# A decoder layer on one core: late operand loads on ScalarE's DMA queue, and plain output copies in ScalarE's fixed order

## The chip, the cores and the metric

The kernel runs on one core of a Trainium2 chip: TensorE (PE), VectorE (DVE), ScalarE (ACT), GpSimd (POOL) and SyncE (SP), which here only issues DMAs. The metric is the device time of one execution in microseconds (us), the median of several runs. Engine names in the profile have a q behind them (SPq, ACTq) where the row is of the engine's instruction queue, such as the issue of a DMA.

## The reference

One decoder layer on 512 tokens, model width 2048, hidden width 5632, all in float32:

```
h = rmsnorm(x);  u, v, q, k, v_att, g_a, g_b = split(h @ W_in)
y_a = u * (tril(W_s) rmsnorm(v) + b)          # in chunks of 128 tokens
y_b = stick_breaking_attention(q, k, v_att)
x  += (sigmoid(g_a) * (y_a @ W_up_a) + sigmoid(g_b) * (y_b @ W_up_b)) @ W_o
x  += (silu(h2 @ W_gate_in) * (h2 @ W_up_in)) @ W_out      # h2 = rmsnorm(x)
x  += sigmoid(rmsnorm(x) @ W_pg) * (p @ W_ple)
```

## The kernel before

**Products.** Everything is kept transposed: a block is 128 partitions (features) by 1024, two tiles of 128 features by 512 tokens side by side. A float32 operand is split into a high and a low part in fp32r, and a product takes three matmuls, high x high, high x low, low x high (`mm3`, L296 to L298). Most products are Strassen products of 2 x 2 blocks with seven multiplications (L701); others are "plain", with eight (L296 to L298). One output block is a *pair* (`Pair`): its products run in PSUM over all operands of the stage and are then combined.

**Operands.** Each stage reads operands that are made once: a float32 block is loaded, ScalarE copies it to the high part (L286; with the norm's gain L548 or L529), VectorE subtracts to get the low part (L287, L549), and for a Strassen operand VectorE also forms sums of its quarters (L534), which are split in the same way. A `plain_form` makes its four plain parts first, so that the first pairs can run as plain products, and loads the block a second time for the sums; a `late_form` makes what its first pair needs. Operands of the later stages come from spilled blocks in HBM: `y_spill` (attention's output, for W_up), `mix` (for W_o), `x1` (for the FFN's input), `hid` (for the FFN's output, in three passes of 8, 8 and 6 blocks) and `x2` (for the last gate). They are fetched by `load` (L523 to L526), whose DMA is L525, on SP's queue. So are the blocks that are read as they are: xT, the spilled gates (gsp), ple, and x1 and x2 for the residual sums.

**Stages** by time: W_in up to about 800 us, W_up to 1025, W_o to 1160, the FFN's input to 2020, its output in three passes to 2180, 2345 and 2465, the last gate to 2645. While the last pair of a stage is computed, the operands of the next one are built.

**Weights.** SP loads each weight block (L339 plain; L341 and L349 for Strassen) into one of a few landings, GpSimd adds two blocks by an accumulating DMA (L370), ScalarE copies the high part (L366), VectorE subtracts the low part (L363) and forms sums (L382). Three slots of high and low parts (whi0 to whi2, wlo0 to wlo2) go round. A landing is free when L363 has read it.

**What sets the order.** A scheduler places the instructions of each engine, with two bounds. `in_turn` chains the instructions given to it in a fixed order on their engine: the weights' L366, L363 and L382, and most of what combines an output. `tick` keeps the instructions of a step behind the newest chained instruction of ScalarE, VectorE and TensorE. SP has no such chain but for its weight loads among themselves (`asked`), so that a load of L525 on SP may stand far ahead of the step that asked for it. `Pair.out` (L793 to L800) copies a plain pair's two PSUM banks to SBUF on ScalarE (L799), outside the chain; a Strassen pair's copies (L724, L757) are in it.

**The start** (L873 to L936): `ple_raw` loads p in two halves on ScalarE's queue (L876), then ScalarE loads its function table (L922), TensorE warms up (L927), SP loads three w_ple blocks (L339), the first block of x (L919) and the gains.

Of the kernel before, what the change touches and what calls it, by code (L numbers as in the profile page):

```python
# [14 lines left out]
AF = mybir.ActivationFunctionType  # L15
# [5 lines left out]
T = 512  # L21
# [49 lines left out]
def hybrid_layer(  # L71
# [18 lines left out]
    nc = tc.nc  # L90
# [358 lines left out]
    def plain_weights(src):  # L449
        return Weights(src.rearrange("p (b c) -> p b c", b=4), 1, "P")  # L450
# [69 lines left out]
    def cut(x):  # L520
        return x.rearrange("p (b c) -> p b c", c=256)

    def load(src, n=1024, how="old"):  # L523
        b = take(n, how)
        nc.sync.dma_start(out=b.f(0, 1024), in_=src)  # L525
        return b  # L526

    def gained(dst, src, gi, k):
# [91 lines left out]
    def plain_form(src, ready=always, gain=None, raw=1024, how="low", far=False):  # L620
        def steps(form):
            hi, lo = form.blocks = parts.take(1024, how), parts.take(1024, how)
            w = form.raw()
            if gain:
                gained(hi.own(), w.f(), *gain)
                gi, k = gain
                for i in range(2):
                    a, b = i * T, (i + 1) * T
                    nc.vector.scalar_tensor_tensor(
                        out=lo.own(a, b), in0=w.f(a, b),  # L630
                        scalar=gcol[:, gi + 2 * k + i : gi + 2 * k + i + 1], in1=hi.f(a, b),
                        op0=ALU.mult, op1=ALU.subtract)
            else:
                split_into(hi.own(), lo.own(), w.f())
            give(w)
            return tuple([x.own(0, T), x.own(T)] for x in form.blocks)
            yield

        return Form("P", steps, [(parts, 1024, how)] * 2 + [(wholes, raw, "low")] * bool(raw),
                    ready, src, far)  # L640

    class Pair:
# [150 lines left out]
        def out(self, o=None):  # L793
            if self.n["S"]:
                assert o is None
                return self.rest(self.o)
            o = wide() if o is None else o
            for i, ps in enumerate(self.ends()):
                nc.scalar.activation(o[:, i * T : (i + 1) * T], ps, AF.Copy)  # L799
            return o  # L800

        def rest(self, o):
# [67 lines left out]
    ple_spill = {}  # L870
    ps_p = []

    def ple_raw(queue):  # L873
        raw = take(1024, "old")
        for k in (0, T):
            queue.dma_start(out=raw.f(k, k + T), in_=pT[:, k : k + T])  # L876
        return raw

    def ple_operands(raw=None):
        first = raw is not None  # L880
        raw = raw or ple_raw(nc.sync)
        ps_p.extend(parts.take(1024, "high") for _ in range(2))
        for k in (0, T):
            ops = split_into(*(x.own(k, k + T) for x in ps_p), raw.f(k, k + T))
            if first:
                in_turn(*ops)
        give(raw)
# [30 lines left out]
        x_raw.append(take(1024, "old"))  # L918
        nc.sync.dma_start(out=x_raw[-1].f(), in_=xT[len(x_raw) - 1])  # L919

    p_raw = ple_raw(nc.scalar)
    nc.scalar.preload_act_table_set("natural_log_exp_and_others")  # L922
    ones = consts.tile([P, P], F32, name="ones")
    nc.vector.memset(ones, 1.0)
    warm = small_bank()
    for _ in range(7):
        nc.tensor.matmul(warm[:, :P], ones, ones, start=True, stop=True)  # L927
    w_early = [plain_weights(w_ple[i]) for i in range(3)]
    load_x()
    gcol = consts.tile([P, ng], F32, name="gcol")  # L930
    nc.sync.dma_start(out=gcol, in_=gains)
# [384 lines left out]
            plan(w_gate[j], now(GATE, GATE_UNTIL, j))  # L1316

    def y_form(c, i):
        return plain_form((lambda: y_a[i]) if c == "a" else lambda: load(y_spill[i]),
                          lambda: len(y_done) == 8, raw=0 if c == "a" else 1024,  # L1320
                          far=c == "b")

# [40 lines left out]

    def spilled_form(kind, n, j, gain=None, **how):
        return (late_form if kind == "S" else plain_form)(
            lambda size=1024: load(spill[n, j], size), lambda: (n, j) in there, gain, far=True,
            **how)

    def store(n, j, block):
# [235 lines left out]
```

## Time and profile before

| | |
|---|---|
| median of 3 runs | 2656.03 us (2655.14 to 2657.5) |
| the profiled execution | 2652.22 us |
| its span in the trace | 2650.5 us, granted clock 0.999 |
| ScalarE busy | 1409.0 us |
| GpSimd busy | 451.5 us |
| DMA queue of SP | 440.77 MB, 50.6% of 16 engines' span |
| DMA queue of GpSimd | 117.47 MB, 27.8% |
| DMA queue of ScalarE | 0.52 MB, 0.1% |

A row of the waits names who waited, at which line, for what, then the total, the number of times and the longest. A row of a timeline has the start in us, the length (of all of them where xN follows), the engine, the line, the operation, out<-in, the form, and in brackets the idle time before it and what ended it. Line numbers are those of the kernel before.

### The profile page before, as it was taken

How to read it: one execution, taken by the hardware profiler on the slowest of the kernel's cores; microseconds unless marked ns; L12 is line 12 of the kernel's file. 1: busy time of each engine (PE TensorE's matmuls, PEld its weight loads, DVE VectorE, ACT ScalarE, POOL GpSimd, SP SyncE). 2: the span in 40 equal slices, each digit the busy share in tenths (PEclk: the TensorE clock that was granted, in tenths of full speed). 3: DMA queues.
4: the chain of work that ended last, by engine and by line, in shares of the span. 5: the costliest groups of instructions: out<-in, count | busy, mean ns of one | idle time of the engine just before them, and what ended most of it. 6: DMA issues, size and time to landing. Idle time of an engine off the chain costs nothing.

```text
span 2650.5 us, 42355 instructions
## 1 busy us (share of the span) xinstructions
PE 2635.0 (99%) x15202; PEld 2301.7 (87%) x15202; DVE 2255.1 (85%) x3856; ACT 1409.0 (53%) x2245; POOL 451.5 (17%) x559
## 2 busy tenths in 40 slices
PE   9999999999999999999999999999999999999999
PEld 7888888889998888888888888888888888889888
DVE  8687878787887558999888888888889989989898
ACT  7756565655554335466444444444445445455543
POOL 0222223232220001101111111111110211211010
PEclk9999999999999999999999999999999999999999
DMA  6777777677775669988888788888887989988794
GB/s 209 183 195 171 194 172 192 171 192 191 175 195 186 223 224 271 254 246 212 223 213 217 197 203 203 195 212 201 202 203 225 255 227 275 225 242 254 239 269 137
DMA packets 288130, 561.46 MB, mean 212 GB/s; under 512 B 26288, under 2 KB 133552, under 8 KB 287920
## 3 DMA queue, kind: packets, MB, share of 16 engines
q1 hardware_dynamic: 225856, 440.77, 50.6%
q0 software_dynamic: 61776, 117.47, 27.8%
q8 instruction: 119, 1.95, 0.3%
q14 instruction: 91, 0.75, 0.1%
q10 hardware_dynamic: 288, 0.52, 0.1%
HBM read 507.28 MB, written 51.38 MB: 211 GB/s over the span
## 4 chain that ended last, share of the span: by engine, by line
PE 94%; DVE 3%; ACT 1%; DMA 1%; issue 1%; SPq 0%; DVEq 0%; ACTq 0%
PE ps L701 56%; PE ps L298 9%; PE ps L297 9%; PE ps L296 9%; PE small L701 6%; DVE wlo L363 1%; PE small L1181 1%; PE small L1129 1%; PE small L1055 1%; DVE parts L287 1%; DVE wholes L534 0%; DVE wholes L382 0%; PE small L1240 0%; DMA wholes<-x 0%; DMA wholes<-w_ffn_out 0%
## 5 line engine op out<-in xcount | busy, mean ns | idle before, releaser
L701 PE MATMUL ps<-parts,whi 128*128 128x512 f32 x4390 | 1470.6, 398 | 1.9 <-DVE out L806 0.8
L366 ACT ACTIVATE whi<-wholes 128x512 fp32r<-128x512 f32 (+2 forms) x934 | 873.1, 948 | 759.4 <-DVE wholes L382 308.6
L363 DVE TENSOR_TENSOR wlo<-wholes,whi 128x512 fp32r<-128x512 f32 (+2 forms) x934 | 980.8, 1086 | 78.5 <-ACT whi L366 77.6
L701 PEld LDWEIGHTS ps<-parts,wlo 128*128 128x128 f32 x4390 | 823.9, 188 | 188.0 <-DVE wlo L363 2.5
L701 PE MATMUL ps<-parts,wlo 128*128 128x256 f32 x4390 | 868.4, 279 | 1.1 <-DVE wlo L363 1.1
L701 PEld LDWEIGHTS ps<-parts,whi 128*128 128x128 f32 x4390 | 707.2, 189 | 11.3 <-issue 3.1
L297 PE MATMUL ps<-parts,whi 128*128 128x256 f32 (+1 forms) x1622 | 538.4, 332 | 1.0 <-DVE parts L287 0.9
L298 PE MATMUL ps<-parts,wlo 128*128 128x256 f32 (+1 forms) x1622 | 538.3, 333 | 1.1 <-DVE wlo L363 1.1
L296 PE MATMUL ps<-parts,whi 128*128 128x256 f32 (+1 forms) x1612 | 532.5, 332 | 1.8 <-ACT parts L286 1.4
L382 DVE TENSOR_TENSOR wholes<-wholes 128x256 f32<-128x256 f32 x820 | 346.3, 422 | 15.8 <-DVE wlo L363 0.4
L760 DVE TENSOR_TENSOR out<-out,ps 128x256 f32<-128x256 f32 x525 | 216.8, 416 | 152.2 <-ACT out L757 152.0
L297 PEld LDWEIGHTS ps<-parts,whi 128*128 128x128 f32 x1622 | 305.9, 189 | 37.9 <-DVE parts L287 2.9
L298 PEld LDWEIGHTS ps<-parts,wlo 128*128 128x128 f32 x1622 | 306.2, 189 | 30.6 <-DVE wlo L363 1.5
L296 PEld LDWEIGHTS ps<-parts,whi 128*128 128x128 f32 x1612 | 303.5, 189 | 32.2 <-ACT parts L286 2.2
L370 POOL DMA_DIRECT2D wholes<-w_ffn_in x169 | 147.6, 873 | 704.2 <-DVE wholes L382 209.7
L370 POOL DMA_DIRECT2D wholes<-w_in x132 | 117.0, 888 | 543.1 <-DMA wholes<-w_in 112.3
L701 PE MATMUL small<-parts,whi 128*128 128x512 f32 x480 | 190.2, 397 | 0.0
L757 ACT ACTIVATE out<-ps 128x256 f32<-128x256 f32 x279 | 104.7, 385 | 57.0 <-PE ps L701 52.9
L287 DVE TENSOR_TENSOR parts<-wholes,parts 128x1024 fp32r<-128x1024 f32 (+3 forms) x139 | 124.0, 904 | 12.6 <-ACT parts L286 12.5
L286 ACT ACTIVATE parts<-wholes 128x1024 fp32r<-128x1024 f32 (+3 forms) x139 | 107.8, 797 | 46.5 <-DVE wholes L534 32.4
L370 POOL DMA_DIRECT2D wholes<-w_ffn_out x64 | 55.9, 873 | 356.0 <-DMA wholes<-w_ffn_out 84.7
L1428 ACT ACTIVATE out<-out 128x512 f32<-128x512 f32 x44 | 27.9, 633 | 156.2 <-DVE out L1427 156.2
(135 smaller groups left out, 1833.6 us busy)
## 6 DMA issues: line engine op xcount, KB each, us to landing
wholes<-w_ffn_in SPq DMA_DIRECT2D x169, 384.0 KB, 5.6
wholes<-w_in SPq DMA_DIRECT2D x132, 384.0 KB, 5.0
wholes<-w_ffn_in SPq DMA_DIRECT2D x169, 256.0 KB, 4.8
wholes<-w_ffn_in POOLq DMA_DIRECT2D x169, 256.0 KB, 5.4
wholes<-w_in SPq DMA_DIRECT2D x132, 256.0 KB, 4.1
wholes<-w_in POOLq DMA_DIRECT2D x132, 256.0 KB, 5.0
wholes<-w_ffn_out SPq DMA_DIRECT2D x64, 384.0 KB, 6.0
wholes<-x SPq DMA_DIRECT2D x46, 512.0 KB, 6.1
```

What stands on the lines that cost most here:

```text
L286: return (nc.scalar.activation(hi, src, AF.Copy), nc.vector.tensor_tensor(out=lo, in0=src, in1=hi.bitcast(F32), op=ALU.subtract))
L287: nc.vector.tensor_tensor(out=lo, in0=src, in1=hi.bitcast(F32), op=ALU.subtract))
L296: nc.tensor.matmul(ps, sh, mh, start=start, stop=False)
L297: nc.tensor.matmul(ps, sh, ml, start=False, stop=False)
L298: return nc.tensor.matmul(ps, sl, mh, start=False, stop=stop)
L363: in_turn(nc.vector.tensor_tensor(out=self.lo[:, blocks], in0=r, in1=h.bitcast(F32), op=ALU.subtract))
L366: in_turn(nc.scalar.activation(h, r, AF.Copy))
L370: nc.gpsimd.dma_start(out=raw[:, 3:5], in_=self.src[:, 1:3], accum_op=ALU.add)
L382: in_turn(nc.vector.tensor_tensor(out=o, in0=x, in1=y, op=ALU.add))
L701: m = nc.tensor.matmul(out, l, r, start=first and k == 0, stop=last and k == 1)
L757: in_turn(nc.scalar.activation(out, x, AF.Copy, scale=scale))
L760: in_turn(nc.vector.tensor_tensor(out=out, in0=x, in1=y, op=op))
```

## The change

Three edits:

```
-    def load(src, n=1024, how="old"):
+    def load(src, n=1024, how="old", queue=nc.sync):
         b = take(n, how)
-        nc.sync.dma_start(out=b.f(0, 1024), in_=src)
+        queue.dma_start(out=b.f(0, 1024), in_=src)
...
-        return plain_form((lambda: y_a[i]) if c == "a" else lambda: load(y_spill[i]),
+        return plain_form((lambda: y_a[i]) if c == "a" else lambda: load(y_spill[i], queue=nc.scalar),
...
-            lambda size=1024: load(spill[n, j], size), lambda: (n, j) in there, gain, far=True,
+            lambda size=1024: load(spill[n, j], size, queue=nc.scalar), lambda: (n, j) in there, gain, far=True,
```

The 92 loads of y_spill, mix, x1, hid and x2 that make operands go to ScalarE's queue; the other loads of L525 stay on SP.

```
             for i, ps in enumerate(self.ends()):
-                nc.scalar.activation(o[:, i * T : (i + 1) * T], ps, AF.Copy)
+                in_turn(nc.scalar.activation(o[:, i * T : (i + 1) * T], ps, AF.Copy))
```

The 16 copies of L799 that go through ScalarE for eight plain pairs join ScalarE's chain.

```
-    def ple_raw(queue):
+    def ple_raw(*queues):
         raw = take(1024, "old")
-        for k in (0, T):
-            queue.dma_start(out=raw.f(k, k + T), in_=pT[:, k : k + T])
+        for k, q in zip((0, T), queues):
+            q.dma_start(out=raw.f(k, k + T), in_=pT[:, k : k + T])
...
-    p_raw = ple_raw(nc.scalar)
+    w_early = [plain_weights(w_ple[0])]
+    p_raw = ple_raw(nc.scalar, nc.sync)
...
-    w_early = [plain_weights(w_ple[i]) for i in range(3)]
+    w_early.extend(plain_weights(w_ple[i]) for i in range(1, 3))
```

At the start the second half of p is loaded by SP, behind the first w_ple block; the second use of `ple_raw`, in the middle of the kernel, keeps both halves on SP.

What the scheduler makes of it. First ScalarE where the operands of the first hid pass are made (2011 to 2024 us), before; whi are weights' high parts, parts are operands, out and p5 are PSUM copies of an output.

```order
L366 ACTIVATE whi0_75<-wholes_74 128x512
L366 ACTIVATE whi2_79<-wholes_74 128x1280
L366 ACTIVATE whi2_79<-wholes_74 128x512
L366 ACTIVATE whi1_77<-wholes_74 128x1024
L286 ACTIVATE parts_73<-wholes_74 128x4x256 x3
L366 ACTIVATE whi0_75<-wholes_74 128x1024
L757 ACTIVATE out_1727_18757<-ps_1711_18637 128x256
```

And changed:

```order
L366 ACTIVATE whi2_79<-wholes_74 128x1280
L525 DMA wholes_74<-hid_1164_10912 128x1024
L366 ACTIVATE whi2_79<-wholes_74 128x512
L525 DMA wholes_74<-hid_1165_10913 128x1024
L366 ACTIVATE whi1_77<-wholes_74 128x1024
L525 DMA wholes_74<-hid_1166_10914 128x1024
L286 ACTIVATE parts_73<-wholes_74 128x4x256
L366 ACTIVATE whi0_75<-wholes_74 128x1024
L525 DMA wholes_74<-hid_1167_10915 128x1024
L286 ACTIVATE parts_73<-wholes_74 128x4x256
L525 DMA wholes_74<-hid_1168_10916 128x1024
L286 ACTIVATE parts_73<-wholes_74 128x4x256
```

The loads of the first five blocks now stand among ScalarE's weight copies of that stretch, each behind the copy before it, and the second and third operand's L286 stand behind the copy to whi0 that they preceded.

SP, before, in the FFN's input stage, where the load of the first hid block is issued at 1221.9 us (hid_10912 on the left is a store of it, on the right the load):

```order
L349 DMA wholes_74<-w_ffn_in 128x768
L1431 DMA hid_1164_10912<-out_1257_11121 128x512
L341 DMA wholes_74<-w_ffn_in 128x2x256
L349 DMA wholes_74<-w_ffn_in 128x768
L525 DMA wholes_74<-hid_1164_10912 128x1024
L341 DMA wholes_74<-w_ffn_in 128x2x256
L349 DMA wholes_74<-w_ffn_in 128x768
```

and in the changed kernel the same stretch of weight loads:

```order
L341 DMA wholes_74<-w_ffn_in 128x2x256
L1432 DMA hid_1164_10912<-out_1257_11121 128x512
L349 DMA wholes_74<-w_ffn_in 128x768
L341 DMA wholes_74<-w_ffn_in 128x2x256
L349 DMA wholes_74<-w_ffn_in 128x768
L341 DMA wholes_74<-w_ffn_in 128x2x256
L349 DMA wholes_74<-w_ffn_in 128x768
```

The load of hid has left it; what remains are weights and the stores of L1431 (L1432).

TensorE, in the first pair of the first hid pass (ps_1739 and ps_1740 are the two banks of its output, whi0 and wlo0 the parts of its weight), before:

```order
L296 MATMUL ps_1739_18816<-parts_73,whi0_75 128x512
L297 MATMUL ps_1739_18816<-parts_73,whi0_75 128x512
L298 MATMUL ps_1739_18816<-parts_73,wlo0_76 128x512
L296 MATMUL ps_1739_18816<-parts_73,whi0_75 128x512
L297 MATMUL ps_1739_18816<-parts_73,whi0_75 128x512
L298 MATMUL ps_1739_18816<-parts_73,wlo0_76 128x512
L296 MATMUL ps_1740_18817<-parts_73,whi0_75 128x512
L297 MATMUL ps_1740_18817<-parts_73,whi0_75 128x512
```

and changed:

```order
L296 MATMUL ps_1739_18816<-parts_73,whi0_75 128x512
L296 MATMUL ps_1740_18817<-parts_73,whi0_75 128x512
L297 MATMUL ps_1739_18816<-parts_73,whi0_75 128x512
L298 MATMUL ps_1739_18816<-parts_73,wlo0_76 128x512
L296 MATMUL ps_1739_18816<-parts_73,whi0_75 128x512
L297 MATMUL ps_1739_18816<-parts_73,whi0_75 128x512
L298 MATMUL ps_1739_18816<-parts_73,wlo0_76 128x512
L297 MATMUL ps_1740_18817<-parts_73,whi0_75 128x512
```

One product of the second bank, which needs only high parts, stands ahead of the product that needs the operand's low part (L297).

More of the change, by code (lines that the diff above doesn't have):

```diff
@@ L880, in ple_operands @@
         first = raw is not None
-        raw = raw or ple_raw(nc.sync)
+        raw = raw or ple_raw(nc.sync, nc.sync)
         ps_p.extend(parts.take(1024, "high") for _ in range(2))
```

## The prediction

> **What bounds the kernel now.** I read the page first: busy time by engine, then the chain of work that ended last.
>
> ```profile
> PE 2635.0 (99%) x15202; PEld 2301.7 (87%) x15202; DVE 2255.1 (85%) x3856; ACT 1409.0 (53%) x2245; POOL 451.5 (17%) x559
> PE 94%; DVE 3%; ACT 1%; DMA 1%; issue 1%; SPq 0%; DVEq 0%; ACTq 0%
> ```
>
> TensorE is busy for 2635.0 of 2650.5 us, so the change can give back 15 us at the very most, and it removes no matmul. It can only move waits. The waits of TensorE, the second view, are the whole stock of possible gain:
>
> ```profile
> PE ps L296 <- ACT parts L286: 1.4, 1, 1.4
> PE small L1129 <- ACT wholes L1078: 1.2, 3, 0.5
> PE small L927 <- DVE expo L947: 1.1, 1, 1.1
> PE ps L701 <- DVE wlo L363: 1.1, 2, 0.9
> PE ps L298 <- DVE wlo L363: 1.1, 1, 1.1
> PE ps L297 <- DVE parts L287: 0.9, 3, 0.5
> PE ps L701 <- DVE out L806: 0.8, 1, 0.8
> PE ps L701 <- ACT whi L366: 0.7, 2, 0.4
> PE ps L701 <- ACT out L799: 0.3, 1, 0.3
> ```
>
> These rows sum to 7.6 us. The operands that the change touches (parts of L286 and L287, the copies of L799) hold 1.4 + 0.9 + 0.3 = 2.6 us of it. So a gain over 0.2% (5.3 us of the median 2656.03, about what a measurement of this kernel can tell from no change) needs two thirds of every wait in the list.
>
> Third, what SP's queue waits for, since the change takes 92 loads off it:
>
> ```profile
> SPq L341 <- DVE wlo L363: 1325.9, 377, 10.0
> ...
> SPq L525 <- DVE parts L287: 49.6, 30, 4.0
> SPq L525 <- DMA x<-wholes: 45.0, 16, 6.2
> ```
>
> SP spends 1325.9 us waiting for VectorE to finish with a weight landing (L363) and 49.6 us in loads of L525 that wait for a buffer. The weights are fetched at the pace at which VectorE frees landings, whether or not SP has other loads in between. At the one place where a weight came late behind the loads of L525 (TensorE waits twice near 2237, 0.9 and 0.4 us), SP's timeline says the same:
>
> ```profile
> 2211.98 6.34 SPq L525 DMA_DIRECT2D wholes<-hid  x3
> 2220.84 0.38 SPq L341 DMA_DIRECT2D wholes<-w_ffn_out  x1
> 2219.60 1.22 DVE L363 TENSOR_TENSOR wlo<-wholes,whi 128x1024 fp32r<-128x1024 f32 x1
> ```
>
> The three loads are through at 2218.32, and the weight load is issued 2.5 us later; what it waited for is the L363 on the same landing, which ended at 2220.82. The queue was free.
>
> Fourth, where operands are made for a new stage, VectorE has no spare time. Busy times in three stretches (span of the window, then TensorE, its loads, VectorE, ScalarE, GpSimd):
>
> ```profile
> 2010.00:2020.00 10.00, 10.00 (x59) 8.73 (x58) 9.95 (x14) 6.86 (x8) 0.00 (x0) 1.00 0.51 148
> 2040.00:2060.00 20.00, 20.00 (x129) 18.21 (x128) 20.00 (x33) 12.21 (x15) 3.54 (x4) 1.00 0.96 287
> 2195.00:2215.00 20.00, 20.00 (x115) 17.61 (x115) 19.97 (x28) 10.72 (x12) 1.76 (x2) 1.00 0.96 281
> ```
>
> A microsecond that VectorE loses at such a border isn't recovered for 20 us or so. TensorE's granted clock is 1.00 in all three.
>
> **The change, part by part.**
>
> *Issue time on ScalarE.* At the start ScalarE issues two DMAs itself, the only ones it has now:
>
> ```profile
> 0.80 0.90 ACTq L876 DMA_DIRECT2D wholes<-pT  x2
> 1.73 1.28 ACT L922 ACT_TABLE_LOAD   x1 [1.73 <-PEq L1595]
> 0.81 1.34 SPq L339 DMA_DIRECT2D wholes<-w_ple  x3
> ```
>
> One issue costs it 0.45 us, and the table load behind them starts only when they are out. 92 loads x 0.45 = 41 us, onto an engine that is busy 1409 of 2650 us: spread evenly this is nothing, and all of it lies at the six borders between stages, 16 loads in some 35 us each (7 us of ScalarE, busy 5 to 7 us in 10 there). It costs what it delays on VectorE, counted below. The Trainium skill ("DMA: Bandwidth & Descriptors", under "Issuing engines are not separate DMA queues") says that DMAs begun by different engines run on the same 16 DMA engines, and that only the sequencer's time is saved by spreading them. By it no load lands sooner; the trace has no load of this size from ScalarE that would test it.
>
> *When the loads start.* This is the larger part. On SP the scheduler hoisted the loads, on ScalarE their place is held by the chain of L366:
>
> ```profile
> L525 SPq DMA_DIRECT2D wholes<-hid x42: 319/326/456, 1221.9 to 2362.6; - x42
> DMA to landing us min/median/max: 3.1/5.5/8.3
> ```
>
> The first hid load was issued at 1221.9 for a pass that begins to read it at 2016. Changed, the order has it behind the L366 that ends at 2013.09:
>
> ```profile
> 2011.83 1.26 ACT L366 ACTIVATE whi<-wholes 128x1280 fp32r<-128x1280 f32 x1
> 2014.59 0.63 ACT L366 ACTIVATE whi<-wholes 128x512 fp32r<-128x512 f32 x1 [1.50 <-DVE wholes L382]
> 2016.36 2.94 ACT L286 ACTIVATE parts<-wholes 128x1024 fp32r<-128x1024 f32 x3
> 2020.27 1.06 ACT L366 ACTIVATE whi<-wholes 128x1024 fp32r<-128x1024 f32 x1 [0.97 <-ACT parts L286]
> 2017.63 3.49 DVE L287 TENSOR_TENSOR parts<-wholes,parts 128x1024 fp32r<-128x1024 f32 x3
> 2022.03 0.42 DVE L760 TENSOR_TENSOR out<-out,ps 128x256 f32<-128x256 f32 x1 [0.91 <-ACT out L757]
> 2031.25 1.22 DVE L287 TENSOR_TENSOR parts<-wholes,parts 128x1024 fp32r<-128x1024 f32 x1
> 2036.70 0.39 PE L297 MATMUL ps<-parts,whi 128*128 128x512 f32 x1
> ```
>
> Issued at 2013.1, landed after the median 5.5 us at 2018.6, so the first L286 runs 2.2 us later than 2016.36. The second and third then stand behind the L366 of 2020.27 and run to 2023.3 where they ended at 2019.3. Two of VectorE's three L287 (3.49 / 3 = 1.16 us each) fall out of the stretch up to 2021.1 and come in after the copies of 2022.03: VectorE is 2 x 1.16 + 0.8 (the part of its idle time that it can't use) = 3.1 us behind. The fifth L287 would then end at 2032.47 + 3.1 = 2035.6, and the matmul that first reads it started at 2036.70: no stall yet. The saturated stretch that follows passes the 3.1 us on to operands with less slack, and TensorE's changed order puts a product of the neighbouring output ahead there (0.23 us from one start to the next, a few of them). Bounds 0 and +3.1; I take **+1.2**, nearer to the first, since the two early slacks cover all of it.
>
> *The second pass (2172 to 2225).* The same with less slack:
>
> ```profile
> 2177.84 2.35 DVE L287 TENSOR_TENSOR parts<-wholes,parts 128x1024 fp32r<-128x1024 f32 x2
> 2182.24 0.42 DVE L760 TENSOR_TENSOR out<-out,ps 128x256 f32<-128x256 f32 x1 [2.05 <-ACT out L757]
> 2189.72 1.22 DVE L287 TENSOR_TENSOR parts<-wholes,parts 128x1024 fp32r<-128x1024 f32 x1
> 2191.47 0.39 PE L297 MATMUL ps<-parts,whi 128*128 128x512 f32 x1
> 2194.74 0.50 PE L297 MATMUL ps<-parts,whi 128*128 128x512 f32 x1 [0.15 <-DVE parts L287]
> ```
>
> One L287 more slips past 2182.24, about 1.6 us with what is left of the 2.05 us gap. The L287 that ended at 2190.94 had 0.5 us in hand before 2191.47, and at 2194.74 TensorE already waits. 1.6 - 0.5 = 1.1 us, and some more at 2194.74: bounds 0 and +2.8, taken **+1.5**. The third pass (12 loads, smaller backlog) by the same steps: 0 to +1.5, taken **+0.7**.
>
> *The loads of x1 and x2, of mix and of y* (32, 16 and 4 less what stays). Between mix and the w_o products a load in ScalarE's order waits for a store of its own block with two PSUM copies behind it; before the x1 stage two loads lose their lead, and the splits of L548 come 3 to 5 us later, with products of other operands pulled ahead on TensorE. No wait of the trace stands there now; the nearest rows for what a late operand costs are the list above, 0.2 to 1.4 us a time. So for each of the four places 0 to one or two such waits: y +0.2, mix +0.5, x1 +0.8, x2 +0.3, together **+1.8**, bounds -1 (a load that SP held back for the next buffer's owner is free to go) and +6.
>
> *The copies of L799 in turn.* 16 instructions of 0.59 us that now keep their place. TensorE waits once for one of them, 0.3 us. Bounds -0.3 and +0.6 (one L366 held behind one copy); taken **-0.3**.
>
> *The start.* Half of pT goes to SP, and the first w_ple load is ahead of it. The first real matmul waits 1.4 us for the L286 that reads pT; ScalarE's table load starts 0.45 us earlier, and the two halves are issued side by side. SP's other loads move back by one issue (1.34 / 3 = 0.45 us). Bounds 0 and -1; taken **-0.4**.
>
> *SP's freed time.* 92 issues of 0.33 us and the waits above leave SP. By the rows on SP it gains where its next load waits for nothing else: bounds 0 and -2, taken **-0.8**.
>
> Sum: 1.2 + 1.5 + 0.7 + 1.8 - 0.3 - 0.4 - 0.8 = **+3.7 us**. The profiled execution took 2652.2 us around its span of 2650.5, so one like it would show 2655.9; that execution lies 3.8 us under the median of 2656.03, and the forecast for the median is 2656.0 + 3.7 = **2659.7 us**.
>
> **The rivals.**
>
> *Slower by more than 0.2%.* The lead of the loads is the kernel's cover, and nothing takes its place: each of the three passes pays its whole VectorE backlog (3.1 + 2.8 + 1.5 = 7.4 us), the other places 2 to 4 more, less 1 at the start and the copies: +8 to +11, about 2666. It decides from the point where TensorE's order has no other ready product when an L287 comes 2 us late. For it: 20.00 of 20.00 us busy on VectorE. Against it: slacks of 2 to 5 us early in the first pass and the reordering on TensorE. The Trainium skill ("DMA: Bandwidth & Descriptors", "Rules for kernel authors") advises to issue a DMA early and wait for it late; that speaks for this case, and the lead of 790 us for the first hid load is the trace's extreme of it.
>
> *Faster by more than 0.2%.* VectorE's 178 sums of L534, 69 us, no longer run ahead of need among the products of the stage before, so weight splits there come on time, and SP, free of waits, fetches every weight a little sooner: 2237, the border at 1047 and the waits for L363 and L366 (1.1 + 1.1 + 0.8 + 0.7), the operand waits (2.6), all gone: -6.3, about 2650. It decides from the point where almost no new wait appears. Against it: SP's queue was not what the weight at 2220.84 waited for.
>
> *The change doesn't reach the time.* Loads land in time, copies were in that order anyway: within 1.5 us of 2656.
>
> **How the numbers follow.** Forecast (a small loss within the threshold, +1.5 to +5.3): 0.36. No effect: 0.20. Slower rival: 0.32. Faster rival: 0.12. The first two make "same", 0.56. The range leaves out about 1 in 10 on each side: down to 2652 (the moved loads cost nothing and the small gains all come), up to 2668 (the rival's full backlog, with a stall or two more).
>
> **What would show it.** Right: ScalarE's queue shows 92 loads of L525 at about 0.45 us; the first hid loads issue after 2010 and the first L286 of that pass comes 2 to 3 us later, relative to TensorE; the waits of TensorE for parts of L286, L287 and L549 grow by 3 to 6 us in total, mostly at the borders of the hid passes; the wait for L799 is gone. Wrong: if these waits don't grow (VectorE's backlog was absorbed), if TensorE's busy time itself changes by more than 2 us, or if waits for L363 and L366 at the weights shrink by more than 2 us (SP was the brake after all).

## The result, and the profile after

The changed kernel takes 2676.05 us (median of 5 runs, 2673.41 to 2679.77) against 2656.03 for the kernel before: a ratio of 1.0074, 95% interval 1.0059 to 1.0088. It is slower by 20 us, where 3.7 were forecast and the range ended at 12 us. The profiled execution is the slowest of the five, 2679.77 us with a span of 2677.9, 27 us over the span of before, whose profiled execution lies 3.8 us under its median.

In the changed kernel the lines from L922 on have a number one higher. First the page's busy times and its chain:

```profile
PE 2643.5 (99%) x15202; PEld 2304.8 (86%) x15202; DVE 2253.9 (84%) x3856; ACT 1407.1 (53%) x2245; POOL 451.4 (17%) x559
PE 91%; DVE 4%; DMA 3%; ACT 1%; issue 1%; POOL 0%; DVEq 0%; ACTq 0%; SPq 0%; POOLq 0%
```

No engine does more work, except that TensorE's busy time is up by 8.5 us with as many matmuls. DMA has 3% of the chain where it had 1%. TensorE's waits:

```profile
PE ps L701 <- ACT whi L366: 4.7, 3, 3.5
PE ps L296 <- ACT whi L366: 3.5, 2, 1.8
PE ps L701 <- DVE out L806: 3.0, 1, 3.0
PE ps L296 <- ACT parts L286: 3.0, 2, 1.7
PE small L1241 <- ACT wholes L1079: 2.9, 1, 2.9
PE ps L701 <- DVE wlo L363: 2.3, 3, 0.9
PE ps L296 <- DVE out L760: 2.1, 2, 1.1
PE ps L297 <- DVE parts L287: 1.8, 5, 0.5
PE ps L298 <- DVE wlo L363: 1.4, 3, 0.9
```

All waits of the list are 28 us, where they were 9: 19 us more, and with the 8.5 us of busy time that makes the 27. Few of the new waits name the operands (L286, L287) whose loads were moved. Most name weights (L366, L363) and combined outputs (L806, L760), which come behind ScalarE's and VectorE's work on those operands; the places below show two cases.

Where the time goes. I compared the starts of TensorE's matmuls in the two traces, the k-th with the k-th, and took the growth of the difference over stretches of the kernel (times of before). The same table holds the experiments; each row is one profiled execution, and "ratio" is that of the timed runs:

| us lost in | to 800 | y 800-840 | mix 840-1060 | x1 1060-1260 | FFN in to 2000 | pass 1 to 2160 | pass 2 to 2340 | pass 3, x2 to 2480 | gate to the end | ratio, interval |
|---|---|---|---|---|---|---|---|---|---|---|
| changed | 4.6 | 0.0 | 4.7 | 2.9 | 0.0 | 5.2 | 1.6 | 5.5 | 2.7 | 1.0074 (1.0059 to 1.0088) |
| loads only | 1.5 | 0.0 | 5.2 | 3.0 | 0.0 | 5.5 | 1.7 | 5.7 | 1.5 | 1.0085 (1.0070 to 1.0101) |
| copies only | 2.2 | 0.1 | -0.5 | 0.0 | 0.0 | 0.0 | 0.4 | -0.2 | -1.3 | 1.0002 (0.9993 to 1.0011) |
| start only | 2.7 | -0.2 | 0.3 | 0.2 | 0.0 | 0.6 | 1.5 | -0.2 | -1.5 | 0.9997 (0.9988 to 1.0005) |
| hid only | 1.2 | 0.0 | 0.3 | 0.0 | 0.0 | 4.1 | 1.4 | 1.3 | -1.7 | 1.0027 (1.0018 to 1.0035) |
| x1, x2 only | 0.4 | 0.9 | -0.4 | 2.9 | 0.0 | 0.4 | 0.0 | 1.7 | 1.4 | 1.0027 (1.0018 to 1.0037) |
| second loads only | 3.8 | -0.1 | 3.7 | 1.8 | 0.0 | 1.8 | 2.4 | -0.2 | 3.3 | 1.0039 (1.0026 to 1.0051) |
| hid, asked a pair earlier | 5.1 | -0.4 | -0.7 | 0.3 | 0.0 | 5.6 | 1.6 | 0.9 | -0.3 | 1.0029 (1.0018 to 1.0041) |
| SP, pinned | 1.0 | 13.5 | 1.2 | 1.2 | 0.0 | 1.3 | 1.9 | 0.8 | 0.2 | 1.0071 (1.0058 to 1.0083) |
| SP, pinned, y free | 5.0 | 0.1 | 0.3 | 1.3 | 0.0 | 1.0 | 1.8 | 3.0 | -0.1 | 1.0014 (1.0006 to 1.0023) |
| ScalarE, not pinned | 4.5 | 0.0 | 6.4 | 1.8 | 0.2 | 0.0 | -0.4 | 0.5 | 2.1 | 1.0032 (1.0020 to 1.0045) |
| ScalarE, three steps earlier | 4.5 | 0.0 | 0.7 | 2.6 | 0.0 | 0.0 | 0.1 | 0.6 | 1.4 | 1.0042 (1.0029 to 1.0054) |
| the same, L806 in turn | 1.7 | 0.1 | 1.1 | 1.9 | 0.0 | 0.7 | -0.7 | 0.2 | 1.5 | 1.0020 (1.0011 to 1.0028) |
| the same, hid only | 2.9 | 0.1 | -0.2 | 0.0 | 0.0 | 0.9 | 0.1 | -0.2 | 0.6 | 1.0004 (0.9995 to 1.0013) |
| mix's last block on SP | 3.5 | 0.0 | 0.2 | 3.0 | 0.0 | 4.8 | 3.5 | 10.1 | 6.6 | 1.0078 (1.0064 to 1.0092) |
| changed, L806 in turn | 2.4 | 0.0 | 2.2 | 3.3 | 0.0 | 5.2 | 0.9 | 3.3 | 1.8 | 1.0081 (1.0068 to 1.0095) |

The first column is no part of the change: executions in which no load moved (copies only, start only) have 2.2 and 2.7 us there too, and it runs from 0.4 to 5.1. Behind 800 us the entries of these two rows reach 1.5 us, so a single entry of that size says nothing by itself. The losses lie where operands are made, and nowhere else: the FFN's long input stage has none.

**Between mix and the W_o products.** ScalarE's timeline of the changed kernel:

```profile
1032.26 0.84 ACT L286 ACTIVATE parts<-wholes 128x768 fp32r<-128x768 f32 x1 [0.20 <-DVE wholes L534]
1038.63 0.33 ACTq L525 DMA_DIRECT2D wholes<-mix  x1
1039.01 1.09 ACT L724 ACTIVATE out<-ps 128x512 f32<-128x512 f32 x2 [5.90 <-DMA x<-wholes]
```

and the chain there:

```profile
1030.04 8.53 DMA x<-wholes
...
1041.12 0.43 DVE out L727
...
1045.56 3.91 DMA wholes<-w_o
...
1056.32 4.93 PE ps L701 x18
```

The load of 1038.63 needs a buffer that a store, issued at 1030.04, reads until 1038.57. It waits in ScalarE's queue, and the two copies L724, which were ready, stand behind it for 5.9 us. VectorE idles 5.5 us on them, frees the buffer for the next weight block late, that block of w_o is loaded at 1045.56, and TensorE waits 3.0 us at 1056 (row L701 <- L806).

**The first pass of hid.** ScalarE's timeline near the end of the border:

```profile
2060.64 0.33 ACTq L525 DMA_DIRECT2D wholes<-hid  x1
2062.19 1.06 ACT L286 ACTIVATE parts<-wholes 128x1024 fp32r<-128x1024 f32 x1 [3.08 <-DVE wholes L534]
2063.15 0.58 ACT L799 ACTIVATE out<-ps 128x512 f32<-128x512 f32 x1
2063.32 1.80 ACTq L525 DMA_DIRECT2D wholes<-hid  x2
2068.82 1.06 ACT L286 ACTIVATE parts<-wholes 128x1024 fp32r<-128x1024 f32 x1 [5.08 <-DVE wholes L534]
```

and its chain:

```profile
2060.64 7.35 DMA wholes<-hid
2068.02 0.77 DVE wholes L534 x2
2068.82 1.07 ACT parts L286
2069.93 0.85 PE ps L296 x3
```

A second load (for the sums) goes out at 2060.64, lands at 2068.0, VectorE sums, ScalarE copies at 2068.82, and TensorE has nothing else from 2068.2 to 2069.93. It is the twelfth of the pass's sixteen loads, and it went out 5.5 us later than the twelfth load of the kernel before (2042.7), measured from where TensorE stands. Only the first six loads of this pass ever had a long lead, of 600 to 790 us; the other ten went out from 2018.9 on in the kernel before too. The issues themselves cost little: the 0.33 us from 2060.64 lie in time in which ScalarE has no operand to copy, and those from 2063.32 within the copy L799 that runs from 2063.15 to 2063.73.

**What a wait costs.** TensorE's granted clock behind that wait (columns as before; the clock is third from the end):

```profile
2066.00:2068.00 2.00, 2.00 (x19) 1.98 (x17) 0.00 (x0) 0.00 (x0) 0.00 (x0) 1.00 0.99 304
2068.00:2070.00 2.00, 0.26 (x3) 0.07 (x1) 1.88 (x5) 1.18 (x2) 0.00 (x0) 1.00 1.04 312
2070.00:2072.00 2.00, 2.00 (x10) 2.00 (x11) 2.00 (x2) 1.77 (x3) 0.00 (x0) 0.53 0.23 86
2072.00:2074.00 2.00, 2.00 (x9) 1.55 (x8) 2.00 (x5) 1.54 (x2) 0.88 (x1) 0.61 0.83 262
2074.00:2078.00 4.00, 4.00 (x26) 3.58 (x26) 4.00 (x9) 1.58 (x3) 0.00 (x0) 1.00 1.01 190
```

A wait of 1.74 us, and then four microseconds at 0.53 and 0.61 of full speed: 2 x 0.47 + 2 x 0.39 = 1.7 us more. The same follows the waits at 1056 (3.0 us; 0.51 for 3.4 us) and at 2548 (3.5 us; 0.53), not the one at 641 (2.9 us; 1.00). Three such stretches cost some 5 us of the 27; this is most of TensorE's extra busy time of 8.5 us. The kernel before has no wait over 1.5 us between its first and its last matmul, and a clock of 0.999 (changed: 0.997).

**The other rows of before.** At the start ScalarE's table load begins earlier, as forecast:

```profile
0.82 0.41 ACTq L876 DMA_DIRECT2D wholes<-pT  x1
1.25 1.28 ACT L923 ACT_TABLE_LOAD   x1 [1.25 <-PEq L1596]
```

SP has fewer loads and waits longer for landings:

```profile
SPq L341 <- DVE wlo L363: 1427.3, 393, 10.1
```

It was 1325.9: the weights come at VectorE's pace, as the prediction had it.

### The profile page after: what moved, and what is told of

Same layout as the page of the kernel before. It is cut to its first block, busy times and chain, and to the rows that moved or that the text cites. A ratio compares the mean times of both kernels' runs of the same rounds, so it can differ in the third digit from the quotient of the medians.

```text
span 2677.9 us, 42311 instructions
## 1 busy us (share of the span) xinstructions
PE 2643.5 (99%) x15202; PEld 2304.8 (86%) x15202; DVE 2253.9 (84%) x3856; ACT 1407.1 (53%) x2245; POOL 451.4 (17%) x559
## 4 chain that ended last, share of the span: by engine, by line
PE 91%; DVE 4%; DMA 3%; ACT 1%; issue 1%; POOL 0%; DVEq 0%; ACTq 0%; SPq 0%; POOLq 0%
PE ps L701 55%; PE ps L297 9%; PE ps L298 9%; PE ps L296 9%; PE small L701 6%; DMA wholes<-hid 1%; DVE wlo L363 1%; DVE parts L287 1%; PE small L1182 1%; PE small L1130 1%; PE small L1056 1%; DMA x<-wholes 1%; DVE wholes L534 0%; ACT whi L366 0%; DVE wholes L382 0%
## 5 line engine op out<-in xcount | busy, mean ns | idle before, releaser
L701 PE MATMUL ps<-parts,whi 128*128 128x512 f32 x4390 | 1472.3, 398 | 8.3 <-ACT whi L366 4.7
L366 ACT ACTIVATE whi<-wholes 128x512 fp32r<-128x512 f32 (+2 forms) x934 | 872.5, 948 | 785.3 <-DVE wholes L382 324.3
L363 DVE TENSOR_TENSOR wlo<-wholes,whi 128x512 fp32r<-128x512 f32 (+2 forms) x934 | 980.3, 1084 | 86.6 <-ACT whi L366 86.2
L701 PEld LDWEIGHTS ps<-parts,wlo 128*128 128x128 f32 x4390 | 824.6, 188 | 190.0 <-DVE wlo L363 5.4
L701 PE MATMUL ps<-parts,wlo 128*128 128x256 f32 x4390 | 870.1, 279 | 2.3 <-DVE wlo L363 2.3
L701 PEld LDWEIGHTS ps<-parts,whi 128*128 128x128 f32 x4390 | 709.7, 189 | 19.2 <-ACT whi L366 6.3
L297 PE MATMUL ps<-parts,whi 128*128 128x256 f32 (+1 forms) x1622 | 539.1, 333 | 1.9 <-DVE parts L287 1.8
L382 DVE TENSOR_TENSOR wholes<-wholes 128x256 f32<-128x256 f32 x820 | 346.5, 423 | 15.8 <-DVE wlo L363 0.5
L297 PEld LDWEIGHTS ps<-parts,whi 128*128 128x128 f32 x1622 | 306.6, 189 | 40.0 <-DVE parts L287 4.8
L760 DVE TENSOR_TENSOR out<-out,ps 128x256 f32<-128x256 f32 x525 | 215.8, 414 | 142.4 <-ACT out L757 142.2
L370 POOL DMA_DIRECT2D wholes<-w_ffn_in x169 | 147.3, 871 | 706.2 <-DMA wholes<-w_ffn_in 239.3
L370 POOL DMA_DIRECT2D wholes<-w_in x132 | 117.1, 889 | 538.6 <-DMA wholes<-w_in 146.8
L701 PE MATMUL small<-parts,whi 128*128 128x512 f32 x480 | 190.2, 396 | 0.0
L287 DVE TENSOR_TENSOR parts<-wholes,parts 128x1024 fp32r<-128x1024 f32 (+3 forms) x139 | 123.7, 903 | 24.1 <-ACT parts L286 24.0
L286 ACT ACTIVATE parts<-wholes 128x1024 fp32r<-128x1024 f32 (+3 forms) x139 | 108.0, 798 | 63.9 <-DVE wholes L534 39.3
L370 POOL DMA_DIRECT2D wholes<-w_ffn_out x64 | 55.7, 871 | 359.1 <-DMA wholes<-w_ffn_out 121.2
```

The lines of the kernel that those rows point to most:

```text
L286: return (nc.scalar.activation(hi, src, AF.Copy), nc.vector.tensor_tensor(out=lo, in0=src, in1=hi.bitcast(F32), op=ALU.subtract))
L287: nc.vector.tensor_tensor(out=lo, in0=src, in1=hi.bitcast(F32), op=ALU.subtract))
L297: nc.tensor.matmul(ps, sh, ml, start=False, stop=False)
L363: in_turn(nc.vector.tensor_tensor(out=self.lo[:, blocks], in0=r, in1=h.bitcast(F32), op=ALU.subtract))
L366: in_turn(nc.scalar.activation(h, r, AF.Copy))
L370: nc.gpsimd.dma_start(out=raw[:, 3:5], in_=self.src[:, 1:3], accum_op=ALU.add)
```

## The experiments

The first expectations set the loads (theory A) against the copies in turn (B) and against a general disorder from any edit (C). For A there were two forms: that the loads cost their lead (A1), or that they cost their place in ScalarE's queue, where what stands behind a load waits with it (A2).

### The parts one by one

**Loads only.** The kernel before with the first edit (the `queue=nc.scalar` lines) alone.

> Only the 92 loads go to ScalarE's queue; copies and start as before. Theory A (the loads carry the loss: their lead is gone, and ScalarE's order waits where they wait): +16 to +20 us, with TensorE falling behind at 1050 (4), 1235 (2.6), 2040 to 2070 (5), 2200 to 2260 (1.6), 2360 to 2410 (2), 2430 and 2550 (3.5 each), as in the changed kernel. Theory B (the copies in turn carry the losses near 2430 and 2550, where plain pairs end): +10 to +13, those two places gone. Theory C (the order of unrelated work is shaken by any of the edits, DMA times with it): any place, also where no load was moved, such as 641.

Measured: 2678.91 against 2654.44 us, ratio 1.0085, more than expected (24 us for 16 to 20). The table's row is that of the changed kernel within 1.2 us at each place behind 800. The loads are the whole change; theory B falls, and with the next two runs C.

**Copies only.** The second edit alone (`in_turn` around L799).

> Only the copies of L799 join the chain. Theory A: within 2 us of before, the 0.3 us wait for L799 gone. Theory B: +5 to +7, with TensorE's waits for L366 and L363 near 2430 and 2550 as in the changed kernel. Theory C: a few us somewhere, not at those places.

Measured: 2655.62 against 2654.44, ratio 1.0002: no effect that can be measured.

**Start only.** The third edit alone.

> Only the start: half of p and the first w_ple block on SP as in the changed kernel. The prediction's step said -0.4 us. The changed kernel lost 1.5 us in its first 100 us (the wait at 25 us was 1.9 instead of 1.2): if the start edit does that, +1 to +2 and all of it before 100 us; if the edit is harmless, 0 or -0.5.

Measured: 2654.91 against 2654.44, ratio 0.9997: none either. Its trace too has some 2 us before 100 us, but that of "copies only" has 1.3 us and that of "second loads only" 2.8 us, without the edit.

**Hid only.**

```
-            lambda size=1024: load(spill[n, j], size), ...
+            lambda size=1024: load(spill[n, j], size, queue=nc.scalar if n == "hid" else nc.sync), ...
```

> Only the 42 loads of hid go to ScalarE's queue. Theory A: +7 to +10, all of it from 2030 to 2410 (5 + 1.6 + 2). The prediction's own step had +3.4 for these three passes. Theory C: losses at other places too, and not these sums.

Measured: 2662.49 against 2654.44, ratio 1.0027 (7 to 8 us), in the three passes (4.1 + 1.4 + 1.3) and not elsewhere.

**x1 and x2 only.** The same with `n in ("x1", "x2")`.

> Only the loads of x1 and x2 for operands go to ScalarE's queue. The changed kernel lost 2.7 us at 1235 and 4.2 and 3 to 4 us near 2410 and 2545, and gained 1.1 near 2500. If the places are independent: +8 to +10. If the losses near 2410 come from the hid passes before them (a backlog handed on): +3 to +6.

Measured: 2661.27 against 2655.24, ratio 1.0027. 2.9 us at x1 as in the changed kernel, 1.7 before 2480 where that had 5.5, and 1.4 in the gate. So some of the loss near 2430 comes with the other loads; the 6 us measured are the upper end of the second expectation.

### Lead or queue

**The loads on SP, but pinned.**

```
+    def load(src, n=1024, how="old", pinned=False):
         b = take(n, how)
-        nc.sync.dma_start(out=b.f(0, 1024), in_=src)
+        d = nc.sync.dma_start(out=b.f(0, 1024), in_=src)
+        if pinned:
+            for e, name in newest.items():
+                if "Act" in str(e):
+                    tc.add_manual_dep(d.ins, name, ...)
```

The 92 loads get `pinned=True`; the dependency orders the scheduler's work and adds no wait on the chip.

> The kernel before, with the 92 loads still on SP, but each kept behind the newest chained instruction of ScalarE, so that none runs ahead (the first hid load stands behind the FFN input's weights, not among them). Theory A1 (the lost lead is the cost): most of the loss stays, +12 to +20, with stalls at the borders of the hid passes near 2040 to 2070 and at 1235. Theory A2 (the place in ScalarE's queue is the cost: what stands behind a load there waits with it, and the scheduler's order of ScalarE and VectorE follows): -1 to +4, no stall of over 1 us at 1050, 1235, 2070, 2407 or 2545.

Measured: 2673.68 against 2655.24, ratio 1.0071, which looks like A1, but the table shows otherwise: 13.5 us of it lie at y, where the changed kernel loses nothing. SP's queue there:

```profile
803.58 0.33 SPq L525 DMA_DIRECT2D wholes<-y  x1
810.46 0.33 SPq L339 DMA_DIRECT2D wholes<-w_up_b  x1
813.08 0.33 SPq L1361 DMA_DIRECT2D gsp<-out  x1
814.21 0.33 SPq L339 DMA_DIRECT2D wholes<-w_up_a  x1
815.34 7.24 SPq L525 DMA_DIRECT2D wholes<-y  x2
```

The second and third loads of y now stand behind weight loads that wait for landings, and go out 12 us after the first. At the other places the loads on SP cost 6.6 us in all.

**The same, with y free.** As above without `pinned` for y.

> As the pinned loads on SP, but the four loads of y run free. In the pinned run 13.5 us were lost between 800 and 840, where the loads of y came late behind weights on SP, and 6 us at all other places. So +5 to +8 if the places are independent: then the 88 other loads, with the same lost lead, cost on ScalarE's queue three times what they cost on SP, and A2 holds for them. +15 or more would say that the lost lead alone does it.

Measured: 2659.89 against 2654.37, ratio 1.0014 (3.7 us). With the long lead gone just as on ScalarE, 88 loads cost 3.7 us on SP and some 22 on ScalarE; the two profiled executions have 7.4 and 22.6 us behind 800. The long lead was not what mattered; A1 in that form falls. The run doesn't separate the queue from a few microseconds of lead: on SP the first hid load went out 5 us earlier than in "loads only" and the twelfth 3 us earlier, measured from where TensorE stands.

**On ScalarE, without the pin.**

```
-            if i.engine in units:
+            if i.engine in units and "DMA" not in type(i).__name__.upper():
```

This is "loads only" with one more edit, in `tick`.

> The 92 loads on ScalarE's queue, without the rule that keeps a load behind the newest chained instruction of ScalarE: six of the first hid loads go out 800 us ahead again, in ScalarE's order; the other loads move by a few places. Theory A1 (lost lead): the losses of the first hid pass (4 to 5.5 us of 22) and some of the others go, +10 to +16 in all. Theory A2 (the place in ScalarE's queue, and the order of ScalarE and VectorE that follows): within 4 us of the 22.5 us that the loads alone cost, first pass included.

Measured: 2664.00 against 2654.37, ratio 1.0032 (8.6 us). All of the loss in passes 1 and 2 is gone, with six first loads of pass 1 gone out 600 to 790 us ahead and five of pass 2 some 100 us. The loss at mix grows to 6.4 us. The total lies under both expectations: the places don't share one cause. In passes 1 and 2 the queue alone costs nothing here.

**Mix's last block on SP.** The changed kernel with `queue=nc.sync if (n, j) == ("mix", 7) else nc.scalar`.

> The changed kernel, with only the two loads of the last mix block back on SP: one of them stood in ScalarE's queue for 5.5 us at 1033 waiting for a store, with two PSUM copies and a weight copy behind it. Theory A2: the loss between 1042 and 1060 (4.4 us) goes, all others stay, so about 2672, +15 to +19 against before. Theory A1: the block arrives as late as before, and the loss there stays within 1 us.

Measured: at mix 0.2 us instead of 4.7. The two copies run as soon as TensorE is done:

```profile
1030.70 0.85 ACT L286 ACTIVATE parts<-wholes 128x768 fp32r<-128x768 f32 x1 [0.20 <-DVE wholes L534]
1031.45 0.58 ACT L724 ACTIVATE out<-ps 128x512 f32<-128x512 f32 x1
1032.21 0.60 ACT L724 ACTIVATE out<-ps 128x512 f32<-128x512 f32 x1 [0.18 <-PE ps L298]
```

The cause at that place is shown: one load that waits in ScalarE's queue. The time did not follow: 2675.77 against 2655.24, ratio 1.0078, no less than the changed kernel's. Its runs spread over 12 us (2672.22 to 2684.17), and the profiled one, the slowest, lost 10.1 us before 2480 and 6.6 in the gate, in the same order of instructions, with a wait of 4.9 us at 2424 and half clock behind it.

**Second loads only.** `queue=nc.scalar if size > 1024 else nc.sync`, y on SP.

> Only the second loads (for the sums of Strassen operands), 42 of the 92, go to ScalarE's queue; first loads and y stay on SP, hoisted. Theory A1 (the lead of the first loads): 0 to +4. Theory A2: the second loads stand among ScalarE's weight copies as in the changed kernel, so their places keep their loss: near 1050 (4.4), 1235 (2.7), 2070 (2 to 4), 2255 (1 to 2), together +9 to +14.

Measured: 2664.79 against 2654.37, ratio 1.0039. Mix keeps 3.7, x1 1.8, pass 2 2.4, the gate 3.3; pass 1 falls to 1.8 and the stretch before 2480 to nothing. A2's sum holds, but first loads have their share in passes 1 and 3.

**Hid asked for a pair earlier.** "Hid only", with `build` one pair earlier.

```
-        if m == KH - 1:
+        if m == KH - 2:
             build(hs[0])
```

> Only the hid loads on ScalarE's queue, and the operands of each hid pass asked for one pair earlier, as far as the buffers allow (three or four of the first loads move ahead by a pair, some 30 us). Theory A1: the loss of 7.2 us of the hid loads falls to 0 to 3. Theory A2: it stays at 5 to 9, since the loads are as many and the queue is the same.

Measured: 2662.79 against 2655.24, ratio 1.0029, as without it and as A2 expected. The first three loads of pass 1 and the first two of pass 2 went out 17 to 20 us earlier than in "hid only", measured from where TensorE stands; pass 1 still lost 5.6. What is late are loads that follow: the twelfth still went out 3.8 us later than in the kernel before.

**All loads three steps earlier.** "Loads only", and in `tick` a DMA is kept behind the chained instruction that was newest three steps ago.

```
+    older = []
...
         last, units = traced()[-1], dict(newest)
+        older.append(units)
+        early = older[max(0, len(older) - 4)]
...
-            if i.engine in units:
+            pins = early if "DMA" in type(i).__name__.upper() else units
+            if i.engine in pins:
                 tc.add_manual_dep(
-                    i, units[i.engine],
+                    i, pins[i.engine],
```

> The 92 loads on ScalarE's queue, each kept behind the newest chained instruction of three steps before, so that each goes out some three steps (5 to 15 us) earlier in the same queue. Theory A1 in its small form (the few us of lead that a load has over its L286, not the 800 us): the 7.2 us of the hid passes fall to 0 to 3, and the 4.3 us near 2420 with them; 1050 stays or grows, since a load for a store still waits in the queue; +8 to +15 in all. Theory A2: the passes keep 6 us or more, +18 to +24.

Measured: 2665.15 against 2654.71, ratio 1.0042 (the row's 9.8 us contain 4.5 from before 800). Pass 1 loses 0.0, pass 2 0.1, the stretch to 2480 0.6, mix 0.7. ScalarE at the first pass (copies of hid are L290 here, weights L370, loads L529):

```profile
2023.16 0.33 ACTq L529 DMA_DIRECT2D wholes<-hid  x1
2024.05 2.94 ACT L290 ACTIVATE parts<-wholes 128x1024 fp32r<-128x1024 f32 x3
2027.96 1.06 ACT L370 ACTIVATE whi<-wholes 128x1024 fp32r<-128x1024 f32 x1 [0.97 <-ACT parts L290]
```

The three first copies run back to back again, ahead of the weight copy, as in the kernel before. Against "loads only" the first hid load goes out 13 us earlier, measured from where TensorE stands (2006 - 8 against 2021 - 10), the next four 5 to 10 us, the later ones up to 5.5 us. Same queue, as many loads, some microseconds of lead: the loss of the passes was that. At mix the loss went too, though the expectation kept it: the last load of mix goes out there with one of the two PSUM copies ahead of it.

**The same, hid only.**

> Only the hid loads on ScalarE's queue, three steps earlier. The run with all 92 loads three steps earlier lost nothing in the three passes, and the runs with only hid there gained 1.0 near 2500. If the few us of lead are the cause in the passes (A1 in its small form): -2 to +1 against before, where the hid loads alone cost 7 to 8. If another load on the queue had a part in it: +3 to +8.

Measured: 2656.22 against 2654.63, ratio 1.0004 (0.9995 to 1.0013). The 7 us of "hid only" are gone. A gain on the kernel before isn't there.

Over these runs the loss of pass 1 goes with the issue of the twelfth load of the pass, whichever the queue (us later than in the kernel before, measured from where TensorE stands, and the loss in the table):

| | twelfth load later by | pass 1 loses |
|---|---|---|
| changed | 5.5 | 5.2 |
| loads only | 5.0 | 5.5 |
| hid only | 4.9 | 4.1 |
| hid, asked a pair earlier | 3.8 | 5.6 |
| SP, pinned, y free | 2.0 | 1.0 |
| second loads only | 1.5 | 1.8 |
| ScalarE, three steps earlier | 1.1 | 0.0 |
| the same, hid only | 0.9 | 0.9 |
| ScalarE, not pinned | 0.4 | 0.0 |

The four other runs in which hid's loads moved fit: 2.3 us later with losses of 0.7 and 1.3, and 5.3 and 5.5 with 5.2 and 4.8.

### The loss in the gate

Near 2545 the changed kernel waits 3.5 us. VectorE's timeline:

```profile
2537.24 1.22 DVE L1491 TENSOR_TENSOR out<-out,wholes 128x1024 f32<-128x1024 f32 x1
2543.11 0.69 DVE L806 TENSOR_TENSOR out<-ps,out 128x512 f32<-128x512 f32 x1 [4.66 <-PE ps L298]
2543.72 1.22 DVE L1497 TENSOR_TENSOR out<-out,wholes 128x1024 f32<-128x1024 f32 x1
2544.85 0.69 DVE L806 TENSOR_TENSOR out<-small,out 128x512 f32<-128x512 f32 x1
2545.45 1.22 DVE L1497 TENSOR_TENSOR out<-out,wholes 128x1024 f32<-128x1024 f32 x1
2546.59 0.88 DVE L382 TENSOR_TENSOR wholes<-wholes 128x256 f32<-128x256 f32 x2
```

The scheduler has put L806, which waits for TensorE's last product of the pair, ahead of the next weights' sums (L382).

**L806 in turn.** The changed kernel with `in_turn` around L806.

> The changed kernel, with the last VectorE instructions of an output (L806) in VectorE's fixed order, which puts them behind the next weights' sums and splits in the last gate again, as in the kernel before. In the changed kernel two of them stand ahead of those, wait 4.7 us for TensorE, and TensorE then waits 3.7 us for L366 at 2548. Theory A2 (the loss near 2545 is the order of VectorE that the scheduler fell into): that place's 3 to 4 us go, the others stay, +16 to +18. Theory A1 (late loads of x2): it stays, +20 or more.

Measured: 2674.61 against 2654.71, ratio 1.0081. The order is the old one, but the wait only splits in two (1.5 us at 2539, 2.1 at 2552), and the stretch from 2520 to 2550 loses 3.2 us as before. VectorE now:

```profile
2530.97 1.22 DVE L1491 TENSOR_TENSOR out<-out,wholes 128x1024 f32<-128x1024 f32 x1
2534.65 2.48 DVE L1497 TENSOR_TENSOR out<-out,wholes 128x1024 f32<-128x1024 f32 x2 [2.46 <-ACT out L1494]
2537.06 0.88 DVE L382 TENSOR_TENSOR wholes<-wholes 128x256 f32<-128x256 f32 x2
```

L382 comes 19.2 us later than its row of the kernel before (2517.89), at a place where TensorE is 16.1 us behind: 3 us too late, with nothing of L806 ahead of it. The place of L806 is not the cause by itself.

**Three steps earlier, L806 in turn.**

> All 92 loads on ScalarE's queue three steps earlier, with L806 in VectorE's fixed order. Near 2545 each of the two by itself kept 3 us of loss: with the earlier loads VectorE still waited 1.1 us for TensorE in L806, with L806 in its place the sums and splits of x2 still ran 3 us late. If these two together are the cause: the loss near 2545 falls to 0 to 1.5, and +6 to +8 in all. If it stays at 3: neither is, and the cause is left open.

Measured: 2660.85 against 2654.63, ratio 1.0020, the best version with all loads on ScalarE. Near 2545 it still loses 3.3 us. Every version with x2's second loads on ScalarE loses 2.7 to 4.8 between 2520 and 2535, after a gain of 1.0 to 1.3 in the 15 us before, and no other does; why, stays open. So does the smaller loss at x1 (1.8 to 3.3 us, with the second loads alone as well).

## Why the prediction was wrong

- **What bounds the kernel** (TensorE, with its few waits as the whole stock of gain; SP held by VectorE's landings): right, though the rows quoted there sum to 8.6 us and not 7.6. Waits on SP for L363 grew when its other loads went.
- **Issue time on ScalarE costs nothing but what it delays**: right, and less than taken: 0.33 us an issue, and 68 of the 92 lie wholly inside the time of a running ScalarE instruction.
- **When the loads start, pass 1 (+1.2), pass 2 (+1.5), pass 3 (+0.7)**: the mechanism was right and the size was off. Pass 1 lost 5.2 us (4.1 with hid only) and pass 3 2.0; pass 2's 1.6 is close to its forecast, but "start only", which moves no load, has 1.5 there, so it confirms little. The step's first instant was off: the first load went out at 2011.4 and not 2013.1, and the first L286 ran 0.1 us later than before, not 2.2. The second ran 4.8 us later, since each copy now waited for its own load (0.8 and 0.9 us). The step counted the first three loads, and let the backlog of VectorE end the matter. It did not follow the queue further: the second loads of the border went out up to 5.5 us later than before, measured from where TensorE stands, and TensorE's wait came from one of them. That the bound of +3.1 was the whole backlog was the mistake. With three steps of lead the passes cost nothing, so the term of the lead was the right one to look at, and it turns on a few microseconds.
- **The loads of x1, x2, mix and y (+1.8, bounds -1 to +6)**: this step failed. The loads took 4.7 us at mix, 2.9 at x1, 5.5 up to 2480 (pass 3 with it) and 2.7 in the gate. Its prices came from waits that the kernel before shows, 0.2 to 1.4 us a time, in a kernel where nothing is late. The prediction had seen that a load in ScalarE's order "waits for a store of its own block with two PSUM copies behind it", and priced it at 0.5 us. The rows to price it by were the store's time to landing (8.5 us in the changed kernel) and the saturated VectorE behind those copies. At mix the cause is shown; at x1, near 2430 and in the gate it stays open.
- **A wait was priced as its length.** No term had the clock: a wait can be followed by 3.4 us at half speed, some 1.7 us each time. The Trainium skill ("TensorE: Matmul & The Clock Gate", "HAM oscillation — how this bites in real kernels") warns of idle gaps of TensorE over about 3.4 us. Here a gap of 1.74 us was enough and one of 2.9 us was not; the measurement decides. Three such stretches are 5 us of 27.
- **Copies (-0.3), start (-0.4), SP's freed time (-0.8)**: copies and start are nothing that can be measured (ratios 1.0002 and 0.9997). No run has SP's freed time by itself; with 42 loads off SP and their losses gone (three steps earlier, hid only) the ratio is 1.0004, so no gain shows.
- **That no load lands sooner** by ScalarE's queue, for which the prediction named the Trainium skill: the median of hid's loads is 5.6 us from issue to landing, where it was 5.5.
- **The rivals**: the slower one came true in direction, near its price in the passes (7.4 us forecast, 5.2 + 1.6 + 2.0 = 8.8 measured) and at more than three times its price elsewhere (14 against 2 to 4). "It decides from the point where TensorE's order has no other ready product": that was so in pass 1. The faster rival falls, since the waits for L363 and L366 grew, and so does "the change doesn't reach the time".
- **What would show it**: waits for L286 and L287 were to grow by 3 to 6 us. They grew by 2.5 (2.3 to 4.8); the waits for L366 and L363 at the weights, for whose growth there was no term, grew from 3.2 to 12.4. The wait for L799 is gone, as forecast. One sign of being wrong came: TensorE's busy time changed by 8.5 us, where 2 were the limit.

## What to carry to other kernels

On an engine that also computes, a DMA issue was cheap here (0.33 us), but its wait stood in that engine's queue (5.9 us at mix): before moving a load there, look up what its buffer is waiting for, and price everything behind it by that transfer's time, not by the issue. A load needs its landing time and a few microseconds more ahead of its use: in the passes some 5 to 13 us more for the first five loads did what 600 to 790 us had done, and a place right behind the preceding work was too late. Where TensorE is always busy, price a stall by its length plus the slow clock that can follow it.

## What the runs showed of the hardware that was not expected

**The clock.** Waits of TensorE of 1.74 us (2070), 3.0 us (1056) and 3.5 us (2548) were followed by a granted clock of 0.51 to 0.53 for some 3.4 us; in the same execution waits of 2.9 us (641) and 1.7 us (2425) were not. In the run with mix's last block on SP a wait of 4.9 us was followed by 0.50.

Not the length of a wait alone decides, but also where it falls. The three slow stretches last 3.41 us each and start at 1056.38, 2070.14 and 2548.00, whole multiples of 3.413 us apart (297 and 140 of them). With the execution cut into such stretches, TensorE was busy for 0.39, 1.67 and 0.07 us of the 3.41 just before the slow ones. The wait at 641 lies across a border (639.95) and leaves 1.77 and 2.20 us busy on its two sides, and that at 2425 leaves 1.74: the clock stayed full. Over all kept traces, each cut at its own slow stretches, 19 stretches at full clock with at most 1.60 us busy were all followed by a slow one, and of some 13,000 with 1.86 us or more none was; in between, around half of the stretch, it went either way 8 times each. That busy time is modelled in the profile, so the border between the two is no sharper than that.

**A DMA issue on ScalarE's queue** took 0.33 us inside the time of the running copy, where the two at the very start of the kernel before, with nothing running, stood one behind the other (0.90 us).
